# Operand pools moved onto one offset, a fourth pair opened early, 1/rms and the first act moved, own tiles for half-length steps

## The chip, the cores and the metric

The kernel runs on one core of one Trainium2 chip. The metric is the device time of one execution in microseconds. The kernel before takes 2276.01 us (median of 3 runs, 2274.84 to 2279.9). The engines are called as the profile calls them: PE multiplies matrices, PEld loads its weights, DVE, ACT and POOL work on tiles, SP issues the transfers.

## What is computed

One layer of a hybrid network on x of 1024 tokens by 1024 channels, all in float32:

```python
x = x + 0.5 * _swiglu(_rmsnorm(x, ffn1_norm), ffn1_wg, ffn1_wu, ffn1_wd)
h = _rmsnorm(x, mix_norm)
proj = h @ w_in                      # 24 blocks of 128 columns and 32 of gates
# four branches (y_a to y_d), merged with sigmoid gates, then:
x = x + merged @ w_out
x = x + 0.5 * _swiglu(_rmsnorm(x, ffn2_norm), ffn2_wg, ffn2_wu, ffn2_wd)

def _swiglu(x, wg, wu, wd):
    return (silu(x @ wg) * (x @ wu)) @ wd      # 1024 -> 2816 -> 1024
```

## The kernel before

**Numbers in two parts.** Every float32 operand of a large product is split into a rounded part hi and a remainder lo, both in the format float32r: ACT copies hi, DVE (or POOL) subtracts to get lo (`split`, L1010). A product takes three matmuls per block of 128 channels: hi by hi, lo by hi, hi by lo. A matmul has weights of 128x128 (the stationary operand) and 512 columns (the moving operand).

**A feed-forward's first half** (`gate_up`, L1236) runs over 22 pairs f of a gate block and an up block of 128 columns. Each pair's two products (gate and up, two halves of the channels, two halves of the tokens) are computed from seven smaller ones instead of eight, as in Strassen's scheme in Winograd's form: A11, S2, A12, S1, S4, A22, S3 (`NAMES`, L985). Each of the seven is 12 matmuls (`one`, L1154), 84 for a pair. The left operands (the moving ones) come from x, scaled by the norm's gain: A11 and A12 are plain halves of x, S1 to S4 sums and differences of quarters of it. They are made once per feed-forward; A11, A12, S2 and S1 lie in the pools h0 and h1, S3, S4 and A22 in xc (`xc_tiles`, L1015). The right operands (the weights) are made for each pair by `prep_gate` (L1127: g, in pool rg) and `prep_up` (L1136: t in rt, u in ru, v in v), from two loads of 512 KB into the three raw buffers.

`first` (L1166) is A11 and a copy of its result to t by ACT (L1170); `second` (L1173) adds A12 to it and copies it by ACT (L1176); `rest` (L1179) is S2, S1, S4, A22, S3 with DVE's additions. `act` (L1202) multiplies by 1/rms (`scale`), takes silu on ACT and multiplies gate by up on DVE, and every second pair `spill` (L1213) writes seven blocks to memory for the second half.

**The opening.** The norm's 1/rms isn't needed until `act`, so products begin on x itself. `left` (L1426) makes the left operands, and opens pairs 0, 1 and 2, that is, runs their A11 and A12 ahead of S2, since S2 needs sums of x. 1/rms is a background job, `rms` (L1102): 32 matmuls of one column (ms, L1098) give the mean square, `rsqrt` (L148) is a chain of 11 small DVE instructions (L152 to L157) behind one addition (L1108), and 16 matmuls (r, L1116) spread it over the partitions, for two ACT copies to `scale`.

**Background jobs** (`Background`, L65) are generators. Each `one` ticks twice (L1164). A generator yields how many ticks it wants to sleep; `finish` runs it to its end at once. In `rms(2, 7)` the means come at the third tick after it was added, r seven ticks later; `gate_up` calls `finish` after pair 0 (L1250), ahead of its `act`.

**A feed-forward's second half** (`down`, L1257) multiplies the activations with wd, again in seven products. Each runs over six steps of two 128-blocks; the sixth has one block, since 22 pairs make 11 blocks of 256. `factors` (L1291) loads and splits a step's two operands (a from memory, b from wd) into the tiles ahi, alo, dhi, dlo. Steps with an even number in the order of all 42 take the four rg tiles, odd ones two of rt and two of ru, and they are made up to two steps ahead (`get`, L1312).

**The mixers** in between multiply h, in the h0/h1 pools again, with 24 blocks of w_in and 32 of gates (`unit`, L207: 24 matmuls for each half of the tokens), beside background jobs for the branches; `product` (L248) is merged @ w_out, with its moving operands in h0/h1 as well.

**What sets the order.** PE's order is that of the source (L1419 asks for it). The instructions of DVE, ACT, POOL and SP are put in order when the program is built, by a planner with its own estimate of durations, which gives a tile's memory to the next tile of its tag when the last reader is done. Each engine then runs its queue in that order.

**Pools.** SBUF is handed out in the order in which pools are opened (L96 to L100): constants, h0 and h1 (eight tiles of 4096 bytes per partition each), norm, then raw, rg, rt and the rest. The norm pool holds y, t and v of `rsqrt`, two tiles each of 64 bytes per partition. All the large tiles are multiples of 512 bytes.

The functions that the change touches:

Of the kernel before, what the change touches and what calls it, by code (L numbers as in the profile page):

```python
# [11 lines left out]
F32R = mybir.dt.float32r  # L12
# [22 lines left out]
class Weights:  # L35


    def __init__(self, nc, ahead):
        self.nc, self.ahead, self.alloc = nc, ahead, None
        self.src, self.got, self.lo_engine = [], {}, []  # L40
        self.issued = 0
# [51 lines left out]
class Net:  # L93
    def __init__(self, ctx, tc, a, cols):
        self.tc, self.nc, self.a = tc, tc.nc, a
        pool = lambda name, **kw: ctx.enter_context(tc.tile_pool(name=name, **kw))  # L96
        self.cpool = pool("const", bufs=1)
        self.hpools = [pool("h0", bufs=8), pool("h1", bufs=8)]
        self.npool = pool("norm", bufs=1)
        self.wide = {k: pool(k, bufs=b, reuse_waits="tile") for k, b in {"raw": 3, "rg": 4, "rt": 2}.items()}  # L100
        self.w, self.wo = Weights(self.nc, 2), Weights(self.nc, 2)
        self.w.alloc = self.wo.alloc = self.weight
        self.bg = Background()
        nc = self.nc
        self.small = self.const("small")
        self.mean_col = self.column("mean_col")
        nc.gpsimd.memset(self.mean_col, 1.0 / D)
        self.cols = cols
        self.eps = self.column("eps")
        nc.gpsimd.memset(self.eps, EPS)  # L110
# [866 lines left out]
class Ffn:  # L977
# [9 lines left out]
    def __init__(self, net, n, es):  # L987
        self.net, self.nc, self.n = net, net.nc, n
        pool = lambda name, bufs: es.enter_context(
            net.tc.tile_pool(name=f"{name}{n}", bufs=bufs, reuse_waits="tile")  # L990
        )
        sizes = {"xc": 12, "ru": 2, "tt": 1, "a": 3, "u": 1, "scale": 1}
        self.narrow = {k: pool(k, bufs) for k, bufs in {"v": 3, "t": 4, "s": 4}.items()}
        self.wide = net.wide | {k: pool(k, bufs) for k, bufs in sizes.items()}
        self.xc = {}
        self.preps, self.raw_gate = {}, {}
        self.gain = net.col(f"ffn{n}_norm")
        self.ms, self.squares = None, {}
        self.opened = {}
# [51 lines left out]
    def left_cross(self, a11, a21):  # L1051

        for kp in range(2):
            self.nc.vector.tensor_tensor(a11[kp], a11[kp], a21[kp], op=ALU.subtract)
            self.scaled(a11[kp], 2 * kp)
        for kp in range(2):
            self.scaled(a21[kp], 2 * kp)

    def left_s2(self, a11, a22):
        self.s2 = [self.t4("xc", f"S2{kp}") for kp in range(2)]  # L1060
# [1 line left out]
            self.scaled_with(self.s2[kp], a22[kp], 4 + 2 * kp, a11[kp], ALU.subtract)  # L1062
        self.left_split("S2", self.s2)

    def left_rest(self, a11, a12, a21, a22):
        for kp in range(2):
            self.scaled_with(a21[kp], a22[kp], 4 + 2 * kp, a21[kp], ALU.add)
        self.left_split("S1", a21)
        for kp in range(2):
            self.scaled_with(a12[kp], a12[kp], 4 + 2 * kp, self.s2[kp], ALU.subtract)  # L1070
        self.left_split("S4", a12)
        self.left_plain("A22", a22, 4)
        self.left_split("S3", a11)
# [102 lines left out]
        self.nc.scalar.copy(g[:, 0], ps)  # L1176
        return g

    def rest(self, f, t, g, x=None):  # L1179

        nc, net = self.nc, self.net
        V = nc.vector

        def ps_of(name):
            ps = net.ps(f"{name}p{f}")
            self.one(ps, f, name)
            return ps

        V.tensor_tensor(t, ps_of("S2"), t, op=ALU.add)
        if g is None:  # L1190
            g = self.second(f, x)
        w = self.t2("t", f"w{f}")
        V.tensor_tensor(w, ps_of("S1"), t, op=ALU.add)
        u = self.t4("u", f"u{f}")
        V.tensor_tensor(u[:, 0], ps_of("S4"), w, op=ALU.add)
        V.tensor_tensor(g[:, 1], ps_of("A22"), t, op=ALU.add)
        ps = ps_of("S3")
        V.tensor_tensor(g[:, 1], ps, g[:, 1], op=ALU.add)  # L1198
        V.tensor_tensor(u[:, 1], ps, w, op=ALU.add)
        return lambda: self.act(f, g, u)  # L1200

    def act(self, f, g, u):  # L1202
        nc = self.nc
        V = nc.vector
        V.tensor_tensor(g, g, self.scale, op=ALU.mult)  # L1205
        nc.scalar.activation(g, g, AF.Silu)  # L1206
        V.tensor_tensor(u, u, self.scale, op=ALU.mult)
        V.tensor_tensor(g, g, u, op=ALU.mult)
        self.acts[f] = g
        if f % 2:  # L1210
            self.spill(f // 2, self.acts.pop(f - 1), self.acts.pop(f))
# [24 lines left out]
    def gate_up(self, also):  # L1236

        net = self.net
        self.acts = {}
        for f in range(NF):  # L1240
            self.prep_up(f)
            self.prep_gate(f + 1)
            if f in self.opened:
                _, t, g = self.opened.pop(f)
                act = self.rest(f, t, g)
            else:
                x, t = self.first(f)
                act = self.rest(f, t, None, x)
            if f == 0:
                net.bg.finish()  # L1250
            act()
            if f == 2:
                also()

# [2 lines left out]
    def down(self, residual, dst, after):  # L1257
        nc, net = self.nc, self.net
        V, mm = nc.vector, nc.tensor.matmul
        n = NF // 2  # L1260
        steps = (n + 1) // 2
# [5 lines left out]
        def load(kh, nh, s):  # L1267
            w = min(2, n - 2 * s)
            t = self.t4(place[kh, nh][s], f"wd{kh}{nh}{s}")
            src = net.a[f"wd{self.n}"][2 * s : 2 * s + w, kh, nh].rearrange("c p t -> p c t")  # L1270
            nc.sync.dma_start(t[:, :w], src)
            raw[kh, nh, s] = t[:, :w]
# [10 lines left out]
        def right(name, s):  # L1283
            at = {"A11": (0, 0), "S2": (0, 0), "A12": (1, 0), "S4": (1, 1), "S3": (0, 1), "A22": (1, 0)}
            if name != "S1":
                return raw[at[name] + (s,)]
            t = self.t4("tt", f"T1{s}")[:, : raw[0, 0, s].shape[1]]
            V.tensor_tensor(t, raw[1, 1, s], raw[0, 0, s], op=ALU.subtract)
            return t

        def factors(name, s):  # L1291
            w = min(2, n - 2 * s)
            i = order.index((name, s))
            if name == "A11":
                load(0, 0, s)
            a = self.t4("raw", f"in{name}{s}")[:, :w]
            nc.sync.dma_start(a, net.a["acts"][self.NAMES.index(name), 2 * s : 2 * s + w].rearrange("c p t -> p c t"))
            for _ in range(2):
                if i and later:
                    load(*later.pop(0))  # L1300
            b = right(name, s)
            tags = ("rt", "rt", "ru", "ru") if i % 2 else ("rg",) * 4
            hi, lo, bhi, blo = (
                self.t4(tag, f"{what}{name}{s}", F32R)[:, :w] for tag, what in zip(tags, ("ahi", "alo", "dhi", "dlo"))
            )
            bs = self.split(b, bhi, blo)
            return self.split(a, hi, lo), bs

        order = [(name, s) for name in self.NAMES for s in range(steps)]
        ready, summed = {}, set()  # L1310
# [30 lines left out]
        def x_of(q, k):  # L1341
            if (q, k // 2) not in loads:
                x = self.t4(X0[k // 2] if q == 1 else "xc", f"res{q}{k // 2}")
                part = residual[k - k % 2 : k - k % 2 + 2, :, q * TH : (q + 1) * TH].rearrange("k p t -> p k t")
                nc.sync.dma_start(x, part)
                loads[q, k // 2] = x
            return loads[q, k // 2][:, k % 2]
# [21 lines left out]
        for i in range(4):  # L1369
            x = x_of(0, i)  # L1370
# [4 lines left out]
        for i in range(4):  # L1375
            add_half(ws[i], beta[i], ts[i])
            x = x_of(0, 4 + i)
            V.tensor_tensor(x, x, ws[i], op=ALU.add)
        alpha = accumulate("S4", new("D"))
        for i in range(4):  # L1380
            x = x_of(0, 4 + i)
# [4 lines left out]
        for i in range(4):  # L1386
            x = x_of(1, 4 + i)
            V.tensor_tensor(x, x, ws[i], op=ALU.add)
        for i in range(4):
            x = x_of(1, i)  # L1390
            V.tensor_tensor(x, x, ts[i], op=ALU.add)
        beta = accumulate("S3", new("E"))
        for i in range(4):
            x = x_of(1, 4 + i)
            add_half(x, beta[i], x)
            done(1, 4 + i)
            x = x_of(1, i)
# [3 lines left out]
        for i in range(4):  # L1401
            x = x_of(1, i)
# [7 lines left out]
def build(ctx, tc, a, cols):  # L1410
    n = Net(ctx, tc, a, cols)
# [14 lines left out]
    def left(ffn, x0, x1, engine, late):  # L1426

        ffn.open(1)
        for i in range(2):
            ffn.open_second(i)  # L1430
        ffn.left_s2(x0[:2], x1[2:])
        ffn.prep_up(0)
        ffn.open(2)
        ffn.open_second(2)
        ffn.add_squares(engine)
        for q, kp in late:
            ffn.square((x0, x1)[q][kp], q, kp)
            ffn.add_squares(engine)
        ffn.left_rest(x0[:2], x0[2:], x1[:2], x1[2:])
        n.bg.add(ffn.rms(2, 7))  # L1440

    with ExitStack() as es:
        n.psums(es, 8, "f1")
        ffn = Ffn(n, 1, es)
        tags = iter(X0 + ("xc",) * 4)
# [7 lines left out]
        x0 = [load(0, 0)]  # L1453
# [8 lines left out]
        x1 = [load(1, k) for k in range(4)]  # L1462
# [8 lines left out]
    with ExitStack() as es:  # L1471
        n.psums(es, 8, "f2")
        ffn = Ffn(n, 2, es)
        tags = iter(X0 + ("xc",) * 4)
        x = {}
# [109 lines left out]
```

## Time and profile before

| | us |
|---|---|
| median of 3 runs | 2276.01 |
| the profiled execution | 2277.5 |
| its span, first to last instruction | 2275.7 |
| PE busy in the span | 2220.4 |
| DVE busy | 1379.8 |
| ACT busy | 875.5 |
| POOL busy | 327.9 |

The busy time of PE counts a matmul from its start to its modelled end, and neighbours overlap, so that a row's duration (some 390 ns) is longer than the distance between two starts. PEclk is the clock that PE was granted, 1.00 being 2.4 GHz and 0.50 1.2 GHz, as a mean over the stretch. A row of the timeline has start, duration, engine, line, operation, the tile written and the tiles read, their shape and their number, and in brackets how long the engine was idle before and what ended that.

### The profile page before, as it was taken

What the parts mean: (1) busy time and instruction counts of PE and PEld (TensorE: products, weight loads), DVE (VectorE), ACT (ScalarE), POOL (GpSimd) and SP (SyncE); (2) the same over time, 40 slices, a digit from 0 to 9 for tenths busy, and PEclk for the clock granted to TensorE, in tenths of its full rate; (3) what the DMA queues carried; (4) which work ended last, traced back from release to release, by engine and by line L of the source; (5) the groups of instructions that cost most, each with busy time, mean ns of one, the idle gap of its engine ahead of it and who ended that gap; (6) DMA issues with size and microseconds to landing.
All of it is one profiled execution on the core that took longest, in us unless ns stands there. A gap on an engine that the chain in (4) does not pass through costs nothing.

```text
span 2275.7 us, 26198 instructions
## 1 busy us (share of the span) xinstructions
PE 2220.4 (98%) x10144; PEld 1779.5 (78%) x10144; DVE 1379.8 (61%) x1925; ACT 875.5 (38%) x1154; POOL 327.9 (14%) x227
## 2 busy tenths in 40 slices
PE   6899999999999999999999999999999999999999
PEld 5688888887777777787777777888778888888777
DVE  8787777776673436314355233035788787777764
ACT  6232233233443533316477454133433333223332
POOL 0000000000003435223343344321100000000000
PEclk8999999999999999999999999999999999999999
DMA  3233232394333122231111222115223232348432
GB/s 142 93 102 106 86 111 91 124 325 149 106 125 112 53 75 78 77 117 65 58 54 45 74 72 88 47 47 181 79 93 115 93 116 93 116 135 318 139 115 93
DMA packets 115196, 245.10 MB, mean 108 GB/s; under 512 B 11264, under 2 KB 23168, under 8 KB 115072
## 3 DMA queue, kind: packets, MB, share of 16 engines
q1 hardware_dynamic: 115072, 243.44, 32.0%
q8 instruction: 79, 1.29, 0.2%
q14 instruction: 45, 0.37, 0.1%
HBM read 181.00 MB, written 62.39 MB: 107 GB/s over the span
## 4 chain that ended last, share of the span: by engine, by line
PE 91%; DVE 6%; ACT 2%; issue 1%; DMA 0%; POOL 0%; SPq 0%; DVEq 0%; ACTq 0%; POOLq 0%
PE X L1162 3%; PE X L1160 3%; PE X L1161 3%; PE S1p L1160 2%; PE S2p L1162 2%; PE S1p L1162 2%; PE S1p L1161 2%; PE S2p L1161 2%; PE S2p L1160 2%; PE S4p L1161 2%; PE S4p L1160 2%; PE S4p L1162 2%; PE S3p L1162 2%; PE S3p L1161 2%; PE A22p L1161 2%; PE S3p L1160 2%
## 5 line engine op out<-in xcount | busy, mean ns | idle before, releaser
L56 POOL TENSOR_TENSOR wlo<-raw,whi 128x1024 fp32r<-128x1024 f32 x56 | 136.4, 2438 | 258.3 <-ACT whi L55 246.7
L1011 ACT ACTIVATE uhi<-gu 128x1024 fp32r<-128x1024 f32 x44 | 46.7, 1062 | 276.4 <-PE S3p L1161 134.4
L55 ACT ACTIVATE whi<-raw 128x1024 fp32r<-128x1024 f32 x72 | 76.0, 1057 | 186.4 <-PE o L261 23.5
L964 DVE TENSOR_TENSOR gt<-gt,wb 128x512 f32<-128x512 f32 x48 | 32.9, 686 | 139.8 <-PE wb L956 80.0
L1011 ACT ACTIVATE ghi<-gu 128x1024 fp32r<-128x1024 f32 x44 | 46.7, 1060 | 164.4 <-DMA gu<-wgu 129.8
L191 POOL TENSOR_TENSOR nm0lo<-res,nm0hi 128x1024 fp32r<-128x1024 f32 x2 | 4.9, 2444 | 648.9 <-ACT nm0hi L190 648.9
L1160 PE MATMUL X<-A11hi,ghi 128*128 128x512 f32 x176 | 71.1, 404 | 9.3 <-ACT ghi L1011 9.3
L965 POOL TENSOR_TENSOR m<-m,gt 128x512 f32<-128x512 f32 x48 | 62.3, 1299 | 122.6 <-DVE gt L964 121.7
L1012 DVE TENSOR_TENSOR dloS<-wd,dhiS 128x1024 fp32r<-128x1024 f32 (+1 forms) x36 | 43.1, 1196 | 59.6 <-ACT dhiS L1011 59.6
L1160 PE MATMUL X<-A12hi,ghi 128*128 128x512 f32 x176 | 70.8, 402 | 7.7 <-ACT t L1170 7.7
L1162 PE MATMUL X<-A11hi,glo 128*128 128x512 f32 x176 | 71.5, 406 | 6.6 <-DVE glo L1012 6.6
L1011 ACT ACTIVATE dhiA<-wd 128x1024 fp32r<-128x1024 f32 (+1 forms) x36 | 35.6, 990 | 107.3 <-PE Ad L1332 53.4
L1011 ACT ACTIVATE dhiS<-wd 128x1024 fp32r<-128x1024 f32 (+1 forms) x36 | 35.6, 989 | 106.9 <-PE Dd L1332 39.1
L1162 PE MATMUL S2p<-S2hi,tlo 128*128 128x512 f32 x176 | 70.2, 399 | 4.2 <-DVE tlo L1012 4.2
L1206 ACT ACTIVATE a<-a 128x1024 f32<-128x1024 f32 x44 | 46.7, 1062 | 65.3 <-DVE a L1205 65.3
L1160 PE MATMUL S1p<-S1hi,thi 128*128 128x512 f32 x176 | 70.7, 402 | 0.0
L1161 PE MATMUL X<-A11lo,ghi 128*128 128x512 f32 x176 | 70.5, 401 | 0.0
L1162 PE MATMUL S1p<-S1hi,tlo 128*128 128x512 f32 x176 | 70.5, 400 | 0.0
L1161 PE MATMUL S1p<-S1lo,thi 128*128 128x512 f32 x176 | 70.4, 400 | 0.0
L1161 PE MATMUL X<-A12lo,ghi 128*128 128x512 f32 x176 | 70.4, 400 | 0.0
L1198 DVE TENSOR_TENSOR a<-S3p,a 128x512 f32<-128x512 f32 x44 | 30.4, 691 | 66.0 <-PE S3p L1162 66.0
L1332 PE MATMUL Ad<-aloA,dhiA 128*128 128x512 f32 x176 | 68.7, 390 | 1.6 <-DVE aloA L1012 1.6
(1209 smaller groups left out, 6895.1 us busy)
## 6 DMA issues: line engine op xcount, KB each, us to landing
gu<-wgu SPq DMA_DIRECT2D x92, 512.0 KB, 3.6
raw<-w_in SPq DMA_DIRECT2D x56, 512.0 KB, 3.5
acts<-s SPq DMA_DIRECT2D x88, 256.0 KB, 2.8
wd<-wd SPq DMA_DIRECT2D x40, 512.0 KB, 6.5
inS<-acts SPq DMA_DIRECT2D x40, 512.0 KB, 3.7
acts<-a SPq DMA_DIRECT2D x66, 256.0 KB, 3.3
inA<-acts SPq DMA_DIRECT2D x30, 512.0 KB, 3.7
res<-x SPq DMA_DIRECT2D x16, 512.0 KB, 7.1
```

What stands on the lines that cost most here:

```text
L55: nc.scalar.activation(hi, raw, AF.Copy)
L56: getattr(nc, self.lo_engine[i]).tensor_tensor(lo, raw, hi.bitcast(F32), op=ALU.subtract)
L964: nc.vector.tensor_tensor(g, g, ps, op=ALU.mult)
L965: nc.gpsimd.tensor_tensor(m, m, g, op=ALU.add)
L1011: self.nc.scalar.activation(hi, src, AF.Copy)
L1012: self.nc.vector.tensor_tensor(lo, src, hi.bitcast(F32), op=ALU.subtract)
L1160: mm(ps, whi[:, s], hi, start=start and k == 0, stop=False, skip_group_check=True)
L1161: mm(ps, whi[:, s], lo, start=False, stop=False, skip_group_check=True)
L1162: mm(ps, wlo[:, s], hi, start=False, stop=k == 3, skip_group_check=True)
L1198: V.tensor_tensor(g[:, 1], ps, g[:, 1], op=ALU.add)
L1206: nc.scalar.activation(g, g, AF.Silu)
L1332: mm(outs[t], whi[:, j, m], alo[:, j], start=False, stop=False, skip_group_check=True)
```

## The change

1. The norm pool is opened ahead of h0 and h1 instead of behind them.
2. Four pairs are opened instead of three; the t pool has five tiles instead of four. The first half of S1's making (a21 times the gain) moves from `left_cross` to a new `left_s1`, called ahead of the sums of squares.
3. `rms(2, 7)` becomes `rms(4, 7)`. `rest` calls `mid` behind S1 for the opened pairs, and `mid` is `acts`: it finishes the background and runs the acts that wait. Pair 0's act is not run behind pair 0 any more.
4. In `down`, a step of one block takes three tiles of v and one of t; the steps of two blocks alternate between rg and rt/ru by their own count. a is split ahead of b.

```diff
         self.cpool = pool("const", bufs=1)
+        self.npool = pool("norm", bufs=1)
         self.hpools = [pool("h0", bufs=8), pool("h1", bufs=8)]
-        self.npool = pool("norm", bufs=1)
...
-        self.narrow = {k: pool(k, bufs) for k, bufs in {"v": 3, "t": 4, "s": 4}.items()}
+        self.narrow = {k: pool(k, bufs) for k, bufs in {"v": 3, "t": 5, "s": 4}.items()}
...
             self.scaled(a11[kp], 2 * kp)
-        for kp in range(2):
-            self.scaled(a21[kp], 2 * kp)
...
-    def left_rest(self, a11, a12, a21, a22):
+    def left_s1(self, a21, a22):
         for kp in range(2):
+            self.scaled(a21[kp], 2 * kp)
             self.scaled_with(a21[kp], a22[kp], 4 + 2 * kp, a21[kp], ALU.add)
         self.left_split("S1", a21)
+
+    def left_rest(self, a11, a12, a22):
...
-    def rest(self, f, t, g, x=None):
+    def rest(self, f, t, g, x=None, mid=lambda: None):
...
         V.tensor_tensor(w, ps_of("S1"), t, op=ALU.add)
+        mid()
...
         self.acts = {}
+        waiting = []
+
+        def acts():
+            net.bg.finish()
+            while waiting:
+                waiting.pop(0)()
+
         for f in range(NF):
             self.prep_up(f)
             self.prep_gate(f + 1)
             if f in self.opened:
                 _, t, g = self.opened.pop(f)
-                act = self.rest(f, t, g)
+                waiting.append(self.rest(f, t, g, mid=acts))
             else:
                 x, t = self.first(f)
-                act = self.rest(f, t, None, x)
-            if f == 0:
-                net.bg.finish()
-            act()
+                waiting.append(self.rest(f, t, None, x))
+            if f:
+                acts()
...
-            tags = ("rt", "rt", "ru", "ru") if i % 2 else ("rg",) * 4
-            hi, lo, bhi, blo = (
-                self.t4(tag, f"{what}{name}{s}", F32R)[:, :w] for tag, what in zip(tags, ("ahi", "alo", "dhi", "dlo"))
-            )
-            bs = self.split(b, bhi, blo)
-            return self.split(a, hi, lo), bs
+            what = [f"{x}{name}{s}" for x in ("ahi", "dhi", "alo", "dlo")]
+            if w == 1:
+                hi, bhi, lo, blo = (
+                    self.t2(tag, x, F32R).rearrange("p (a b) -> p a b", a=1) for tag, x in zip(("v", "v", "v", "t"), what)
+                )
+            else:
+                full = i - i // steps
+                tags = ("rt", "rt", "ru", "ru") if full % 2 else ("rg",) * 4
+                hi, bhi, lo, blo = (self.t4(tag, x, F32R) for tag, x in zip(tags, what))
+            return self.split(a, hi, lo), self.split(b, bhi, blo)
...
         for i in range(2):
             ffn.open_second(i)
+        ffn.open(2)
         ffn.left_s2(x0[:2], x1[2:])
         ffn.prep_up(0)
-        ffn.open(2)
-        ffn.open_second(2)
+        ffn.open(3)
+        for i in (2, 3):
+            ffn.open_second(i)
+        ffn.left_s1(x1[:2], x1[2:])
         ffn.add_squares(engine)
...
-        ffn.left_rest(x0[:2], x0[2:], x1[:2], x1[2:])
-        n.bg.add(ffn.rms(2, 7))
+        ffn.left_rest(x0[:2], x0[2:], x1[2:])
+        n.bg.add(ffn.rms(4, 7))
```

## Rows read from the trace of the kernel before

**Rows 1.** The page's first part: busy us, share of the span and instructions of each engine.
```profile
PE 2220.4 (98%) x10144; PEld 1779.5 (78%) x10144; DVE 1379.8 (61%) x1925; ACT 875.5 (38%) x1154; POOL 327.9 (14%) x227
```

**Rows 2.** Stretches: length; busy PE, PEld, DVE, ACT, POOL; PEclk, DMA share, GB/s.
```profile
0.00:50.00 50.00, 31.07 (x117) 23.38 (x117) 44.89 (x85) 36.09 (x48) 0.34 (x6) 0.89 0.44 161
50.00:100.00 50.00, 43.23 (x182) 35.81 (x182) 37.40 (x59) 15.28 (x17) 0.00 (x0) 0.87 0.22 79
...
200.00:250.00 50.00, 50.00 (x218) 40.61 (x217) 41.55 (x54) 15.65 (x20) 0.00 (x0) 1.00 0.36 123
...
1600.00:1650.00 50.00, 45.35 (x203) 36.36 (x202) 41.12 (x51) 22.59 (x27) 5.13 (x2) 0.97 0.24 74
1650.00:1700.00 50.00, 47.36 (x207) 38.51 (x206) 42.26 (x60) 17.76 (x20) 0.00 (x0) 0.97 0.33 105
```

**Rows 3.** PE's groups by form, 120 to 460 us: count | busy us, mean ns | idle.
```profile
L1160 PE MATMUL S2p<-S2hi,thi 128*128 128x512 f32 x72 | 28.4, 395 | 0.0
...
L1160 PE MATMUL S3p<-S3hi,uhi 128*128 128x512 f32 x71 | 27.6, 389 | 0.0
```

**Rows 4.** Timeline of PE, 200 to 222 us, one steady pair.
```profile
202.24 0.40 PE L1160 MATMUL S2p<-S2hi,thi 128*128 128x512 f32 x1
...
210.63 0.39 PE L1160 MATMUL S4p<-S4hi,uhi 128*128 128x512 f32 x1
...
213.37 0.39 PE L1160 MATMUL A22p<-A22hi,vhi 128*128 128x512 f32 x1
...
218.81 0.40 PE L1160 MATMUL X<-A11hi,ghi 128*128 128x512 f32 x1
```

**Rows 5.** Timeline of PE, 1450 to 1458 us: twelve of a unit, then the next.
```profile
1449.78 0.40 PE L215 MATMUL gb2q<-nm1hi,whi 128*128 128x512 f32 x1
...
1452.58 0.39 PE L954 MATMUL wb<-ybhi,wbhi 128*128 128x512 f32 x1
```

**Rows 6.** PE's groups by form over the whole span: the output product.
```profile
L260 PE MATMUL o<-mhi,whi 128*128 128x512 f32 x128 | 50.6, 395 | 0.0
```

**Rows 7.** Timeline, 555 to 566 us: a joint between two products of down.
```profile
562.28 1.22 DVE L1012 TENSOR_TENSOR aloS<-inS,ahiS 128x1024 fp32r<-128x1024 f32 x1
...
562.38 0.39 PE L1331 MATMUL Cd<-ahiS,dhiS 128*128 128x512 f32 x1
...
563.56 0.50 PE L1332 MATMUL Cd<-aloS,dhiS 128*128 128x512 f32 x1 [0.79 <-DVE aloS L1012]
563.90 0.40 PE L1333 MATMUL Cd<-ahiS,dloS 128*128 128x512 f32 x1
```

**Rows 8.** Waits of PE, 0 to 130 us: us in total, times, longest.
```profile
PE r L1116 <- DVE f1rs_y L157: 6.8, 1, 6.8
PE X L1162 <- DVE glo L1012: 5.9, 3, 4.9
...
PE S2p L1162 <- DVE tlo L1012: 1.5, 1, 1.5
```

**Rows 9.** Waits of PE, 1600 to 1710 us.
```profile
PE X L1160 <- ACT t L1170: 3.9, 2, 2.4
PE S2p L1162 <- DVE tlo L1012: 2.6, 1, 2.6
```

**Rows 10.** Timeline of DVE, first opening: the chain's first and last instruction.
```profile
54.70 0.16 DVE L1108 TENSOR_SCALAR v<-ms 128x8 f32<-128x8 f32 x1
...
69.74 0.16 DVE L157 SCALAR_TENSOR_TENSOR f1rs_y<-f1rs_t,f1rs_y 128x8 f32<-128x8 f32 x1
```

**Rows 11.** Timeline of DVE, second opening: first, two in the middle, last.
```profile
1643.30 0.17 DVE L1108 TENSOR_SCALAR v<-ms 128x8 f32<-128x8 f32 x1 [3.21 <-PE ms L1098]
...
1650.57 0.17 DVE L155 TENSOR_TENSOR f2rs_t<-f2rs_y 128x8 f32<-128x8 f32 x1
1650.77 0.17 DVE L156 SCALAR_TENSOR_TENSOR f2rs_t<-f2rs_t,v 128x8 f32<-128x8 f32 x1
...
1652.26 0.16 DVE L157 SCALAR_TENSOR_TENSOR f2rs_y<-f2rs_t,f2rs_y 128x8 f32<-128x8 f32 x1
```

## The prediction

> **What bounds the kernel now.** The page comes first: PE is busy for 2220.4 us of 2275.7 [rows 1], so the time is what the matmuls take plus some 55 us in which PE stands. The table by stage says where it stands [rows 2]: in the first 100 us (18.9 and 6.8 us) and again where the second feed-forward opens (4.6 and 2.6 us), there also at a lower granted clock (0.89 and 0.87, then 0.97), while 200 to 250 us shows 50.00 of 50.00 at 1.00, with DVE at 41.6. So a change gains either where PE stands or in what one matmul takes, and I asked for both.
>
> A matmul's duration overlaps its neighbour's, so the cost of one is the distance between starts. In a steady pair, the 36 matmuls from 202.24 to 210.63 (S2, A12, S1) are 233.1 ns apart, and the 24 of A22 and S3, from 213.37 to 218.81, 226.7 ns [rows 4]. The groups by form say the same as 395 and 389 ns [rows 3]. All have 128x128 weights, 512 columns and the full clock. What sets the 395 ns group apart is the pool of the moving operand: A11, A12, S2, S1 lie in h0/h1, those of 389 ns in xc. The mixers' units, whose moving operand lies in h0/h1 too, show 2.80 us for 12, that is 233.3 ns [rows 5], and the output product 395 ns [rows 6].
>
> **The change, part by part.** The sum is made against the profiled execution (2277.5 us, span 2275.7). It stands 1.5 us above the median of 2276.0, and I give the result against the median.
>
> *1. The norm pool ahead of h0/h1.* It holds six tiles of 16 floats, 384 bytes. Before, h0/h1 lie ahead of it and every other operand pool behind it, so the two operands of the 395 ns group differ by 384 bytes (less whole multiples of 512), and those of the other by none. Afterwards none differ. The group counts: 2 feed-forwards x 22 pairs x 4 products x 12 = 2112; 56 units x 2 halves x 24 = 2688; the product 2x2x4x24 = 384; together 5184. At 233.1 - 226.7 = 6.4 ns that is 33.2 us. In the two openings (4 pairs each, 384 matmuls) other engines set the pace, so I count 4800: **-30.7 us**. The units of [rows 5] follow each other without a gap, so I let their 2688 count in full. Bounds: 0 (the cause is something else about these pools) and -33.2. I take the upper part, because down draws both operands from several pools and its first row in [rows 7] is 0.39 us long as well, so the weights' pool isn't the cause. What remains open is whether it's the offset or the place of h0/h1 itself.
> The trace has two speeds for one shape [rows 4]. The Trainium skill, "TensorE: Matmul & The Clock Gate", section "Step-by-step: what each phase is for", says that PE reads SBUF through two independent ports, one for the moving operand and one for the weights. By that, where the two lie should not matter, and this term would be 0.
>
> *2. Own tiles for down's half-length steps.* Each product of down ends in a step of one block (12 matmuls, 2.7 us instead of 5.4), and the next product's first step needs the tiles of the step before that. Its alo is written last: DVE starts it at 562.28, PE has begun at 562.38, and the second matmul comes at 563.56, 1.18 us after the first, with 0.34 more behind it, instead of 2 x 0.227 [rows 7]. That is 1.06 us. The same stands at each of the six joints of either feed-forward, 12 in all: 12.7 us. With v, v, v, t for the half step and the parity counted over full steps, the next full step takes tiles that came free one step earlier, 5.4 us. Then DVE's two splits (1.22 us each [rows 7]) fit, and ACT's two, which run beside them. The order a before b makes alo earlier by one more. One of the 12 joints lies beside the first feed-forward's norm, where DVE and POOL are taken by it, and may stay: **-12 us** (-8 to -13). What hides the added tile: t has five, four hold dt, and v is free in down.
>
> *3. The openings.* (a) A fourth pair's A11 and A12, 24 matmuls or 5.6 us, come ahead of the first S2. They don't go away: they are taken from pair 3. They are worth what they cover, at most the waits in the X matmuls: 5.9 us on glo in the first opening [rows 8], 3.9 us on ACT's copy of t in the second [rows 9]. But A11 of pair 3 needs its own glo, behind pair 0's up part on DVE, where pair 2's stood before: I take half, -5 us in all. Its cost on the queues: one more 512 KB load per feed-forward on SP's queue (the opened gate is read again) and one more split at prep time that was done later before. A fourth gate result finds no free tile of a (three) until pair 0's spill is out, so one of eight PSUM banks stays taken till then; a pair needs five: 0. (b) The four scalings of a21 no longer stand ahead of the t copies on ACT's queue: -2, of the 4.8 us that (a) leaves of these waits. On POOL, which adds the squares in the second opening, nothing is added: 0. (c) tlo is late at the first unopened pair: PE waits 1.5 us and 2.6 us at S2 [rows 8, 9]. DVE and the three raw buffers then run behind, since an opened pair has only 60 matmuls, 13.8 us. That wait moves one pair on: 0.
> (d) *1/rms.* By its name it comes later. I read the code otherwise. rms(4, 7) gets its first four ticks from S2 and S1 of pair 0, which leave its counter at 1. Then pair 0's own mid() drains the background, with nothing waiting yet. So the 32 small ms matmuls and r stand on PE together, between S1 and S4 of pair 0, and PE waits for the whole chain on DVE. Behind r stand S4, A22, S3 of pair 0 and all that DVE and ACT make of them. Price: the chain's first instruction to its last took 15.0 us in the first opening, with other work of DVE between its steps, and 9.0 in the second [rows 10, 11]; where nothing came between, a step took 0.20 us [rows 11], and 11 steps 2.2. Before, 42 matmuls (9.8 us) lay between, and r waited 6.8 us and none. In its place now stand between 2 and 15 us in each. I take 6 and 5, since DVE has less left to do then and the splits of S1 come earlier. What it gives back: the 6.8 us. A standing PE also pays with its clock: 0.87 over 50 us means 13 us at 1.2 instead of 2.4 GHz, 6.5 us lost [rows 2]. The first opening has such stretches already, the second gets one more like its present one (0.97 over 50 us: 3 us at the lower level, 1.5 lost), about 2 us. (e) The first act, three DVE instructions of 1.22 us, goes behind S1 of pair 1; its transfers leave with pair 1's as before. PE's 13.8 us per pair cover it: 0.
> Sum of 3: -5 + (6 - 6.8) + 5 + 2, about +1; with (b) **-1 us**, from -21 (every wait of rows 8 and 9 gone, no new one) to +21 (15.0 + 9.0 - 6.8 + 4 for the clock, and nothing gained).
>
> Sum: -30.7 - 12 - 1 = -44, so 2276 - 44 = **2232 us**.
>
> **Rivals.** *A. The offset is not the cause* (h0/h1's own region is, or what reads them): part 1 gives 0, 2276 - 13 = 2263 us. For it: no row shows h0/h1 at the other offset. Against: two speeds that follow the pool in three stages [rows 3 to 6]. 0.12. (The Trainium skill's two ports, cited above, would make it this one.) *B. The drained chain costs its whole length*: 15 and 9 us and 4 for the clock, while (a) and (b) still give 7: part 3 comes to +14, and the time to 2248 us. For it: before, DVE put other work between the steps. Against: with PE standing, DVE runs out of such work. 0.14. *C. The openings go as they are meant to*: glo, t, r and tlo waits all vanish, 5.9 + 6.8 + 1.5 + 3.9 + 2.6 = 20.7: 2276 - 30.7 - 12 - 20.7 = 2213 us. That needs the chain to be short, 0.11. *D. Slower: DVE's new order.* The order of DVE's queue is planned anew. If in the steady pairs an act's 3.7 us stood ahead of tlo, as at pair 3 now, each of the 36 unopened pairs would lose 1.5 to 2.6 us [rows 8, 9], 54 to 94 us: 2286 to 2326 us. It decides from 44/36 = 1.2 us per pair. Against: DVE is busy for 41.6 of 50 us with PE never waiting [rows 2], and a pair takes 19.0 us afterwards, against 16.1 of DVE. 0.05.
>
> **How the numbers follow.** The forecast has 0.58, with a range of its own of 2221 to 2243. A and D lie outside of 2212 to 2254, the rest within. About 0.2% (4.6 us) is what a measurement of this kernel can tell from no change. A, B, C and the forecast are all faster by more; D is slower. A and B together would come to 2276 - 12 + 14 = 2278, about 0.12 x 0.14 = 0.02 for the same: faster 0.93, same 0.02, slower 0.05.
>
> **What would show it.** Part 1: X, S1, S2 at 389 ns and starts 226.7 ns apart, units and o alike; 395 would be A. Part 2: no wait on alo at the first step of a product. Part 3: ms and r next to each other between S1 and S4 of pair 0, a PE wait on f1rs_y of 2 to 15 us in both openings, and the wait on tlo at S2 of pair 4. The prediction is wrong if r stands behind pair 0, if the h0/h1 matmuls keep their distance, or if steady pairs show waits of PE.

## The result, and the profile after

The changed kernel takes 2249.47 us (median of 4 runs, 2247.78 to 2251.35) against 2276.67 us (2274.84 to 2279.9) of the kernel before in the same series: a ratio of 0.9879, 95% interval 0.9862 to 0.9896, or 27.2 us less. The forecast was 44 us less. The profiled execution took 2247.78 us with a span of 2246.0, 29.7 less than before. Where they lie, by the starts of the same PE instructions in both traces:

| stretch of PE | before, us | after, us | change |
|---|---|---|---|
| first X to the last matmul of pair 3 | 7.62 to 121.75 | 7.60 to 122.32 | +0.6 |
| to the first matmul of down (18 pairs) | to 470.58 | to 465.27 | -5.9 |
| first down, to the first unit | to 693.99 | to 677.29 | -11.4 |
| mixers, to the output product | to 1523.62 | to 1496.17 | -10.8 |
| output product | to 1613.21 | to 1583.21 | -2.6 |
| second opening, to the last matmul of pair 3 | to 1707.28 | to 1689.41 | +12.1 |
| to the first matmul of down (18 pairs) | to 2056.10 | to 2032.35 | -5.9 |
| second down, to the end | to 2275.70 | to 2245.97 | -6.0 |

The page's first part answers to [rows 1]: PE is busy for 28.7 us less; the others differ by under 3 us.

```profile
PE 2191.7 (98%) x10144; PEld 1782.3 (79%) x10144; DVE 1377.5 (61%) x1925; ACT 873.0 (39%) x1154; POOL 327.3 (15%) x227
```

The table by stage answers to [rows 2], with the same columns.

```profile
0.00:50.00 50.00, 36.04 (x136) 27.54 (x136) 43.27 (x82) 34.63 (x46) 0.34 (x6) 0.93 0.49 172
50.00:100.00 50.00, 39.59 (x181) 33.60 (x181) 37.90 (x60) 17.36 (x22) 0.00 (x0) 0.86 0.23 76
200.00:250.00 50.00, 50.00 (x223) 41.39 (x222) 42.15 (x55) 16.09 (x20) 0.00 (x0) 1.00 0.34 121
1600.00:1650.00 50.00, 41.39 (x184) 34.48 (x183) 31.62 (x50) 17.15 (x22) 0.00 (x0) 0.83 0.19 62
1650.00:1700.00 50.00, 46.20 (x193) 37.22 (x192) 44.81 (x60) 15.71 (x18) 0.00 (x0) 0.93 0.38 126
```

In 200 to 250 us PE fits 223 matmuls in where it had 218. In 1600 to 1650, in the second opening, which begins 30 us earlier than before, it stands for 8.6 us, and its clock is 0.83.

PE's groups by form, 120 to 460 us, answer to [rows 3]; the timeline rows under them to [rows 4]; then the output product over the whole span, to [rows 6].

```profile
L1161 PE MATMUL S3p<-S3hi,uhi 128*128 128x512 f32 x72 | 28.0, 389 | 0.0
...
L1163 PE MATMUL X<-A11hi,glo 128*128 128x512 f32 x72 | 28.0, 389 | 0.0
L1161 PE MATMUL S2p<-S2hi,thi 128*128 128x512 f32 x72 | 28.0, 389 | 0.0
```
```profile
201.43 0.39 PE L1161 MATMUL S2p<-S2hi,thi 128*128 128x512 f32 x1
...
202.11 0.39 PE L1161 MATMUL S2p<-S2hi,thi 128*128 128x512 f32 x1
```
```profile
L260 PE MATMUL o<-mhi,whi 128*128 128x512 f32 x128 | 49.8, 389 | 0.0
```

The two speeds are gone: all groups show 389 ns, and three S2 matmuls take 0.68 us, 227 ns each. The joint between two products of down [rows 7] has no wait left:

```profile
555.19 0.39 PE L1343 MATMUL Cd<-ahiS,dhiS 128*128 128x512 f32 x1
555.41 0.39 PE L1344 MATMUL Cd<-aloS,dhiS 128*128 128x512 f32 x1
```

The waits of PE in the openings, first 0 to 130 us [rows 8], then 1575 to 1700 us [rows 9]:

```profile
PE X L1161 <- ACT ghi L1011: 11.1, 3, 7.6
PE r L1117 <- DVE f1rs_y L157: 10.4, 1, 10.4
PE X L1163 <- DVE glo L1012: 2.9, 4, 1.8
PE S2p L1163 <- DVE tlo L1012: 2.2, 1, 2.2
PE S2p L1161 <- ACT thi L1011: 1.9, 1, 1.9
```
```profile
PE r L1117 <- DVE f2rs_y L157: 4.6, 1, 4.6
PE X L1161 <- ACT t L1171: 2.6, 1, 2.6
PE X L1163 <- DVE glo L1012: 2.6, 2, 1.8
PE X L1161 <- ACT ghi L1011: 2.1, 1, 2.1
PE S2p L1161 <- ACT thi L1011: 1.9, 1, 1.9
PE S2p L1163 <- DVE tlo L1012: 1.9, 1, 1.9
```

In the first opening glo went from 5.9 to 2.9 us and ACT's t from 3.8 to nothing, while ghi went from 9.3 to 11.1: X waits 14.0 us in all instead of 19.0. In the second, X waits 7.3 us instead of 4.7 (0.8 of that for glo), and ghi is new there. These are the two rows of before, 0 to 130 us, that [rows 8] leaves out:

```profile
PE X L1160 <- ACT ghi L1011: 9.3, 2, 7.6
PE X L1160 <- ACT t L1170: 3.8, 2, 3.1
```

The wait for r grew in the first opening, from 6.8 to 10.4, and is new in the second; the wait for thi in S2 is new in both. PE's timeline shows where r stands, and DVE's the chain (answering to [rows 10]):

```profile
48.33 3.63 PE L1099 MATMUL ms<-mean_col,sq 128*128 128x1 f32 x32
62.37 3.78 PE L1117 MATMUL r<-c_ident,f1rs_y 128*128 128x128 f32 x16 [10.41 <-DVE f1rs_y L157]
65.80 0.77 PE L1161 MATMUL S4p<-S4hi,uhi 128*128 128x512 f32 x1
```
```profile
51.36 2.73 DVE L1030 SCALAR_TENSOR_TENSOR A22lo<-n1x,c_small,A22hi 128x512 fp32r<-128x512 f32 x4
54.01 2.35 DVE L1012 TENSOR_TENSOR S3lo<-n0x,S3hi 128x1024 fp32r<-128x1024 f32 x2
...
56.88 0.15 DVE L1109 TENSOR_SCALAR v<-ms 128x8 f32<-128x8 f32 x1
...
62.14 0.17 DVE L157 SCALAR_TENSOR_TENSOR f1rs_y<-f1rs_t,f1rs_y 128x8 f32<-128x8 f32 x1
```

1/rms doesn't come later. ms and r stand on PE between S1 and S4 of pair 0, as the code was read, and the means, done at 51.96, wait for DVE's splits of A22 and S3 before the chain begins.

### The profile page after: what moved, and what is told of

It reads as the page before. It is cut to its first block, busy times and chain, and to the rows that moved or that the text cites. A ratio compares the mean times of both kernels' runs of the same rounds, so it can differ in the third digit from the quotient of the medians.

```text
span 2246.0 us, 26117 instructions
## 1 busy us (share of the span) xinstructions
PE 2191.7 (98%) x10144; PEld 1782.3 (79%) x10144; DVE 1377.5 (61%) x1925; ACT 873.0 (39%) x1154; POOL 327.3 (15%) x227
## 4 chain that ended last, share of the span: by engine, by line
PE 89%; DVE 6%; ACT 2%; issue 2%; POOL 1%; DMA 0%; SPq 0%; POOLq 0%; ACTq 0%; DVEq 0%
PE X L1163 3%; PE X L1161 3%; PE X L1162 3%; PE S2p L1163 2%; PE S2p L1161 2%; PE S2p L1162 2%; PE S4p L1161 2%; PE Ad L1345 2%; PE S4p L1163 2%; PE S1p L1161 2%; PE S4p L1162 2%; PE Ad L1344 2%; PE S1p L1162 2%; PE S1p L1163 2%; PE Ad L1343 2%; PE S3p L1161 2%
## 5 line engine op out<-in xcount | busy, mean ns | idle before, releaser
L1011 ACT ACTIVATE ahiS<-inS 128x1024 fp32r<-128x1024 f32 (+1 forms) x48 | 46.9, 989 | 131.3 <-PE Dd L1344 31.7
L1012 DVE TENSOR_TENSOR aloS<-inS,ahiS 128x1024 fp32r<-128x1024 f32 (+1 forms) x48 | 54.5, 1135 | 60.9 <-ACT ahiS L1011 60.9
L1161 PE MATMUL X<-A11hi,ghi 128*128 128x512 f32 x176 | 71.9, 409 | 13.2 <-ACT ghi L1011 13.2
L1161 PE MATMUL S2p<-S2hi,thi 128*128 128x512 f32 x176 | 70.2, 399 | 3.8 <-ACT thi L1011 3.8
L1162 PE MATMUL S2p<-S2lo,thi 128*128 128x512 f32 x176 | 70.1, 399 | 0.0
L1161 PE MATMUL S4p<-S4hi,uhi 128*128 128x512 f32 x176 | 69.4, 394 | 0.0
L1162 PE MATMUL S4p<-S4lo,uhi 128*128 128x512 f32 x176 | 68.7, 391 | 0.0
L1163 PE MATMUL S4p<-S4hi,ulo 128*128 128x512 f32 x176 | 68.7, 390 | 0.0
L1345 PE MATMUL Ad<-ahiA,dloA 128*128 128x512 f32 x176 | 68.7, 390 | 0.0
```

What stands on the lines that cost most here:

```text
L1011: self.nc.scalar.activation(hi, src, AF.Copy)
L1012: self.nc.vector.tensor_tensor(lo, src, hi.bitcast(F32), op=ALU.subtract)
L1161: mm(ps, whi[:, s], hi, start=start and k == 0, stop=False, skip_group_check=True)
L1162: mm(ps, whi[:, s], lo, start=False, stop=False, skip_group_check=True)
L1163: mm(ps, wlo[:, s], hi, start=False, stop=k == 3, skip_group_check=True)
L1345: mm(outs[t], wlo[:, j, m], ahi[:, j], start=False, stop=last, skip_group_check=True)
```

## The experiments

Each is compared with the kernel before on its own chip; a gain is the difference of those two medians.

**Each part alone, and the change without its openings.** e1 swaps the two lines of the pools and no more:

```diff
+        self.npool = pool("norm", bufs=1)
         self.hpools = [pool("h0", bufs=8), pool("h1", bufs=8)]
-        self.npool = pool("norm", bufs=1)
```

> The kernel before with the norm pool ahead of h0 and h1 and nothing else. My theory: the offset between the two operands sets 226.7 or 233.1 ns between starts, so this edit alone gives what the comparison of the two traces shows in the steady pairs (36 x 0.33 = 12 us), the mixers (11 us) and the output product (2.6 us), about -25 us, and the S2 and X matmuls show 389 ns. Rival: the shorter matmuls came with another part of the change (other orders, other tiles), and this edit alone gives within 3 us of nothing, with 395 ns as before.

2252.74 us, ratio 0.9895 (0.9878 to 0.9912): 23.2 us less. S2, X and o show 389 ns. By the same starts as in the table, the two times 18 pairs give 5.9 us each, the output product 2.6, the mixers 8.4 and the two openings 2.3 and 0.7; the first down is 2.8 us longer, at a mean clock of 0.98 where before had 1.00. This edit alone does it; the rival falls.

e2 takes only the last hunk of the change, `factors`, and `"t": 5`.

> The kernel before with down's own tiles for the steps of one block (and a split ahead of b, five t tiles) and nothing else. My theory: the wait for alo goes at all joints, and the stretches of down become as short as the two traces show, 11.4 and 6.2 us: -17 us. Rival: only the waits that the prediction counted go, 12 x 1.06 = -12 us, and the rest of what down gained came from other parts of the change.

2258.77 us, 0.992 (0.9905 to 0.9934): 17.2 us less. In its trace the second down is 6.2 us shorter, that is 1.03 us for each of six joints, nearly the 1.06 that the prediction gave one. The first is 9.3 us shorter: from E's first matmul to F's first, beside the norm, it is 3.7 us less, where another product gives some 1.1. Its second opening is 3.7 us shorter as well, with a clock of 0.98 against 0.96 there; no part of the prediction has that.

e3 is the kernel before with parts 2 and 3 of the change's list (openings, 1/rms, act, `"t": 5`).

> The kernel before with the new openings alone: four pairs opened, S1's first half later, 1/rms and the first act moved, five t tiles. My theory: PE stands behind S1 of pair 0 for the whole chain of 1/rms in both openings, and this part costs what the two traces show, 0.6 + 12.1 = +13 us. Rival, the prediction's own term: -1 us, and the loss in the openings comes from how the new orders meet the other two parts.

2293.75 us, 1.0074 (1.0058 to 1.0091): 17.8 us more. By itself this part makes the kernel slower, and its waits are those of the changed kernel (r 10.1 and 4.6 us). By starts its two openings cost 0.3 and 12.6 us, near what my theory said; 5.0 more are lost in the mixers.

e4 is the other half, e1 and e2 together, with the openings of before.

> The changed kernel with the openings of before: norm pool first and own tiles, three pairs opened, 1/rms as before. My theory: the two parts add up and nothing is given back, -25 - 17 = -42 us against before, about 2234 us, some 15 us faster than the changed kernel. Rival: the openings' loss stays although their edit is gone, because the orders of DVE and ACT are planned anew, and it comes out within 5 us of the changed kernel's 2249 us.

2235.59 us (2230.97 to 2238.41), 0.9816 (0.9799 to 0.9833): 40.3 us less, where e1 and e2 sum to 23.2 + 17.2 = 40.4. The two parts add up, and the openings cost the changed kernel 40.3 - 27.2 = 13 us; by starts e4's second opening is 1.7 us shorter than before's, where the changed kernel's is 12.1 longer. The interval lies wholly below the changed kernel's.

**Which part of the openings costs it.** All of these have e1's and e2's edits. In e5 the call behind S1 of pair 0 leaves the background alone:

```diff
         def acts():
-            net.bg.finish()
+            if waiting:
+                net.bg.finish()
```

> The changed kernel, but the call behind S1 of pair 0 finishes the background only when an act waits for it, so that 1/rms runs at its ticks: means in S4 of pair 0, r at the end of S2 of pair 1. My theory: the early draining is what makes PE stand (r waits 10.4 and 4.6 us); 42 matmuls then lie between means and r as before, both waits go almost, and it gains 10 to 14 us on the changed kernel, to about 2237 us. Rival: the chain comes late on DVE wherever r stands, the wait only moves to r at its new place, and it gains at most 3 us.

2241.83 us, 0.9848 (0.9832 to 0.9864): 34.2 us less, 7 better than the changed kernel. No wait for r is left, but a new one, PE on ACT's thi, 5.1 us at S2 of pair 1 in the first opening. The gain lies between the two theories: r's waits went, as mine had it, and the new one took 5.1 of their 15.0 us back.

e6 has the four pairs and S1's later half, but `rms(2, 7)`, and finishes and acts behind pair 0 as before.

> Norm pool, own tiles, four pairs opened and S1's first half later, but 1/rms and the first act as before. My theory: four pairs alone cost about 6 us, nearly all in the second opening, where gate splits stand on ACT's queue behind S1, u and t (X phase 10.4 us longer for 5.5 us of work), so about 2242 us, 6 above the kernel without the new openings (2235.6). Rival: all of the openings' loss is the drained chain, and this comes out at 2231 to 2236 us, as the prediction's -5 and -2 for these edits would have it.

2240.4 us, 0.9842 (0.9827 to 0.9857): 35.6 us less, 4.7 worse than e4.

e7 is the converse, three pairs with the drained 1/rms (the edit against e4):

```diff
         V.tensor_tensor(w, ps_of("S1"), t, op=ALU.add)
+        mid()
...
+                waiting.append(self.rest(f, t, g, mid=acts))
...
-        n.bg.add(ffn.rms(2, 7))
+        n.bg.add(ffn.rms(4, 7))
```

> Norm pool, own tiles, three pairs opened as before, but 1/rms and the first act as in the changed kernel, drained behind S1 of pair 0. My theory: the drained chain costs 1 us net in the first opening and 6 in the second, so about 2243 us, 7 above the kernel without the new openings. Rival: with three pairs opened DVE has more left to do when the chain is asked for, and it costs the 14 us of the whole difference, 2249 us.

2242.56 us, 0.9851 (0.9837 to 0.9866): 33.5 us less, 6.9 worse than e4. With 4.7 from e6 that is 11.6 of the 13. The interval of e7 lies above e4's; that of e6 overlaps it a little.

e11 is e6 with S1's first half where it was before, so that the fourth pair is alone:

> Norm pool, own tiles and four pairs opened, but S1's first half, 1/rms and the first act as before. My theory: the fourth pair alone costs the 5 us, since its split of g stands on ACT's queue ahead of what S2 needs or behind it, so about 2240 us as with S1 moved. Rival: the move of S1's first half costs them (S1's splits come ahead of g's on ACT), and without it this is 2231 to 2235 us, the -5 that the prediction gave the fourth pair.

2242.0 us, 0.9848 (0.9832 to 0.9864): 33.7 us less, 6.6 worse than e4, with an interval that just touches e4's. The traces say where: by starts e11 is 1.0 us shorter than e4 in the first opening and 8.7 longer in the second. So it is the fourth pair by itself that costs time there; S1's move gives back 1.9, which these intervals (some 3.7 us to either side) can't tell from nothing.

Why a fourth pair costs time shows in the changed kernel's second opening. Rows of PE's timeline in 1580 to 1640 us, then DVE's and ACT's beside them:

```profile
1603.17 0.53 PE L1161 MATMUL X<-A11hi,ghi 128*128 128x512 f32 x1 [2.15 <-ACT ghi L1011]
1605.97 0.80 PE L1163 MATMUL X<-A11hi,glo 128*128 128x512 f32 x1 [1.84 <-DVE glo L1012]
1630.22 3.78 PE L1117 MATMUL r<-c_ident,f2rs_y 128*128 128x128 f32 x16 [4.61 <-DVE f2rs_y L157]
```
```profile
1594.17 1.21 DVE L1012 TENSOR_TENSOR S2lo<-S,S2hi 128x1024 fp32r<-128x1024 f32 x1
...
1599.44 1.21 DVE L1012 TENSOR_TENSOR tlo<-tt,thi 128x1024 fp32r<-128x1024 f32 x1
...
1601.18 2.34 DVE L1012 TENSOR_TENSOR S1lo<-o1x,S1hi 128x1024 fp32r<-128x1024 f32 x2
...
1604.71 1.21 DVE L1012 TENSOR_TENSOR glo<-gu,ghi 128x1024 fp32r<-128x1024 f32 x1
```
```profile
1601.06 0.59 ACT L1171 COPY t<-X 128x512 f32<-128x512 f32 x1 [1.77 <-PE X L1163]
...
1602.07 1.05 ACT L1011 ACTIVATE ghi<-gu 128x1024 fp32r<-128x1024 f32 x1
```

S2 of pair 0 needs S2lo and tlo: both are done by 1600.65. But on PE A11 of pair 3 stands ahead of it, and that waits until 1603.17 for ghi, whose split stands on ACT behind the copy of pair 2's t, and until 1605.97 for glo, behind S1lo on DVE. The early pair doesn't fill PE's wait; it puts work that isn't ready ahead of work that is. In e4 PE waits only for t there, 2.58 and 1.02 us. e11 has the same two new waits, 2.1 us for ghi and 1.6 for glo.

**1/rms at its ticks, with three pairs.** e8 is e7 with e5's edit.

> Norm pool, own tiles, three pairs opened as before, 1/rms four ticks in and finished only when an act waits, the first act behind S1 of pair 1. My theory: this is what the move of 1/rms can give by itself, the 6.8 us wait on f1rs_y of the first opening, so about 2229 us, faster than both kernels. Rival: the later act pushes DVE's tlo of pair 3, PE waits there instead, and it stays at 2234 to 2238 us.

2237.25 us (2226.69 to 2240.4), 0.9833 (0.9817 to 0.985): 38.8 us less, not better than e4. Its trace has no wait for r, but this one (waits of PE, 0 to 130 us; then DVE's timeline):

```profile
PE S2p L1160 <- ACT thi L1011: 5.1, 1, 5.1
```
```profile
56.38 0.16 DVE L1108 TENSOR_SCALAR v<-ms 128x8 f32<-128x8 f32 x1
56.57 0.69 DVE L1196 TENSOR_TENSOR u<-S4p,w 128x512 f32<-128x512 f32 x1
...
65.23 0.68 DVE L1146 TENSOR_TENSOR tt<-gu,tt 128x512 f32<-128x512 f32 x1
```

The additions of pair 0 and the chain now lie ahead of pair 1's tt on DVE, and thi needs tt. The rival's number came, by a wait that neither theory had named: thi of pair 1, not tlo of pair 3.

e12 is e8 with `left_s1` as in the change.

> Norm pool, own tiles, three pairs opened, 1/rms at its ticks, the first act behind S1 of pair 1, and S1's first half later as in the changed kernel. My theory: S1's move takes four scalings off ACT's queue ahead of the copies of t and gives the 2 us that the prediction gave it, about 2235 us against 2237 without it, faster than both kernels. Rival: it puts S1's splits where gate splits are waited for and costs 2 us or more, 2239 us and up.

2236.2 us, 0.9824 (0.9809 to 0.9838): 39.5 us less, 0.7 better than e8, which is within the spread. e4, e8 and e12 (2235.6 to 2237.3) all beat both kernels and can't be told apart; e4 is the simplest.

**What about the offset makes the two speeds.** e9 shifts every pool behind norm by two tiles of 64 bytes:

```diff
         self.npool = pool("norm", bufs=1)
+        self.ppool = pool("pad", bufs=1)
         self.hpools = [pool("h0", bufs=8), pool("h1", bufs=8)]
...
+        for i in range(2):
+            nc.gpsimd.memset(self.ppool.tile([P, LINE], F32, tag=f"pad{i}", name=f"pad{i}")[:, :1], 0.0)
```

> The changed kernel with 128 bytes of padding behind the norm pool: h0/h1 lie at 256 modulo 512, where they lay before, and all other operand pools are shifted by as much, so the two operands of a product still differ by nothing modulo 512. My theory: only the difference between the two operands counts; X, S2, S1 and the units stay at 389 ns, and the time is the changed kernel's, 2249 us. Rival: the place of h0/h1 itself sets the speed, and they show 395 ns again, some 25 us more.

One run, 2251.98 us. PE's groups by form, 120 to 460 us:

```profile
L1166 PE MATMUL X<-A11hi,glo 128*128 128x512 f32 x72 | 28.0, 389 | 0.0
L1166 PE MATMUL S2p<-S2hi,tlo 128*128 128x512 f32 x72 | 28.0, 389 | 0.0
```

The h0/h1 pools lie where they lay before, and their matmuls are short all the same: the place itself doesn't matter. e10 puts y and t of the norm, 256 bytes, behind h0/h1 and leaves v ahead:

```diff
         self.hpools = [pool("h0", bufs=8), pool("h1", bufs=8)]
+        self.npool2 = pool("norm2", bufs=1)
...
-        return self.npool.tile([P, LINE], F32, tag=tag, name=name, bufs=bufs)[:, :w]
+        at = self.npool2 if tag[-1] in "yt" else self.npool
+        return at.tile([P, LINE], F32, tag=tag, name=name, bufs=bufs)[:, :w]
```

> The changed kernel with two of the norm pool's three pairs of tiles behind h0/h1 and one ahead, so that the operands differ by 256 bytes modulo 512 instead of by nothing (the kernel before: by 128). My theory: any difference makes them slow, X, S2, S1 and the units show 395 ns, and it takes about 25 us more than the changed kernel, 2274 us. Rival: only the distance of before is slow, and they stay at 389 ns.

One run, 2249.49 us, and the same view shows

```profile
L1163 PE MATMUL X<-A11hi,ghi 128*128 128x512 f32 x72 | 28.0, 389 | 0.0
...
L1163 PE MATMUL S2p<-S2hi,thi 128*128 128x512 f32 x72 | 28.0, 389 | 0.0
```

My theory falls in this form: operands 256 bytes apart are as fast as operands that are alike. What is shown is that 384 bytes between the pools (counted the other way round, 128 modulo 512) are slow and that 0 and 256 are fast. Other distances weren't tried, so the rule behind it stays open.

## Why the prediction was right, and where it was wrong

The sign held, and 2249 lies between the 2212 and 2254 that hold the forecast with B and C. It lies outside of the forecast's own 2221 to 2243: that missed by 17 us. Term by term:

| term | predicted | measured | from |
|---|---|---|---|
| 1, norm pool | -30.7 | -23.2 | e1 |
| 2, own tiles | -12 | -17.2 | e2 |
| 3, openings | -1 | +13.1 | e4 against the changed kernel |
| 3a, fourth pair | -5 | +6.6 | e11 against e4 |
| 3b, S1's half later | -2 | -1.9, -0.7 (not resolved) | e6 against e11, e12 against e8 |
| 3d, 1/rms | +6 - 6.8 + 5 + 2 = +6.2 | +6.9 | e7 against e4 |

**Term 1** was right in its cause and in the size of one matmul. Where PE is fed without a gap the gain came whole: 18 pairs gave 5.9 us, the output product 2.6 (384 x 6.4 ns = 2.5). The step that failed is "I let their 2688 count in full". Of those 17.2 us the mixers gave 8.4 in e1 and 10.8 in the changed kernel. PE's order there is the same in all three traces, so that each distance between two starts can be compared. Of the units' matmuls, 2585 have less than 260 ns to the next start both before and after the change; they came 5.1 ns closer, not 6.4, 13.2 us in all. Of these, 2.4 are lost again: PE stands for 5.9 us instead of 3.3, and these two waits for DVE are new in the changed kernel (waits of PE, 677 to 1496 us).

```profile
PE nm1ms L167 <- DVE work L205: 0.9, 1, 0.9
PE p0q L216 <- DVE nm1lo L191: 0.6, 1, 0.6
```

In e1 the clock takes a share as well: three units come 1.5, 1.9 and 1.7 us later behind the unit ahead of them than they did before, and what comes ahead of two of them lies in these windows, in which before had a clock of 1.00:

```profile
850.00:860.00 10.00, 9.92 (x66) 7.52 (x65) 9.32 (x24) 3.67 (x7) 6.44 (x5) 0.87 0.17 66
...
890.00:910.00 20.00, 19.83 (x105) 14.70 (x103) 13.21 (x38) 3.88 (x6) 9.65 (x7) 0.91 0.19 66
```

The Trainium skill, "TensorE: Matmul & The Clock Gate", section "Step-by-step: what each phase is for", lets PE read both operands through independent ports, from which the prediction drew that this term would be 0. e1 doesn't agree with that: 23.2 us came from moving 384 bytes.

**Term 2** was right in mechanism, to 1.03 against 1.06 us per joint in the second down. The joint that "may stay" didn't: beside the norm PE had more to lose than at the others, and the first down gave 3.1 us more than the second. Some of e2's 17.2 us isn't the joints: the two downs gave 15.5, and the shorter second opening has a part in it.

**Term 3a is the step that failed**, "I take half, -5 us in all". In the first opening it held as far as it went: X waited 5.0 us less, 24 more X matmuls fit ahead of S2, and S2 of pair 0 began at 42.89 us instead of 42.51. But what pair 3 no longer had to do was lost again at its own S2. In the second opening X didn't fill waits but made them, as the rows above show. Of the 8.7 us that e11 loses there against e4, 3.7 are the waits for ghi and glo and 2.5 more waiting at pair 3's S2, with 1.0 less for t; the other 3.5 fit the clock, 0.92 in the mean of that stretch against 0.94. I had priced the waits that a fourth pair could cover, and not that its own splits come last on two queues. One gain I didn't see either: the first down takes 212.0 us with four pairs opened and 214.1 with three (the changed kernel and e4), because PE no longer waits 1.9 us for ACT at the first unit; why ACT is ready sooner is open.

**Term 3c**, "that wait moves one pair on: 0", was wrong in place and size. It stayed at pair 3, although that pair was opened, with thi added to tlo: 1.9 + 2.2 us and 1.9 + 1.9, against 1.5 and 2.6, and a slow stretch behind it. A likely reason, not tested: its A11, 12 matmuls or 2.7 us, no longer stands between pair 2 and its S2.

**Term 3d** was right in place and sign; that its sum fits is partly luck. In the first opening r waited 10.4 us in the changed kernel and 8.6 in e7, where I took 6; in the second 4.6 in both, where I took 5. The 2 us for the clock don't show: by starts e7's openings are 0.9 and 4.9 us longer than e4's, 5.8 in all, where r's waits alone come to 8.6 - 6.8 + 4.6 = 6.4.

**The rivals.** A fell with e1, and h0/h1's own place as the cause with e9; D didn't come: no steady pair waits. B gave 2248 us, and 2249 was measured, but not for B's reason: the drained chain costs 6.9 us and not the +21 that B's +14 was made of; the fourth pair made up the rest, and terms 1 and 2 missed in opposite directions. A total that fits can hide two errors, and only e6, e7 and e11 told them apart. C would have needed a chain without a wait; e5 and e8 have that, and the wait came up elsewhere.

**The clock** is what 2 us in the sum stood for. One stall and what follows it, pair 3 in the first opening (windows with the columns of [rows 2]; then PE's timeline):

```profile
100.00:105.00 5.00, 2.97 (x12) 1.80 (x10) 4.97 (x8) 2.25 (x3) 0.00 (x0) 1.00 0.08 32
105.00:112.00 7.00, 4.95 (x12) 3.91 (x13) 5.15 (x6) 1.44 (x2) 0.00 (x0) 0.51 0.21 78
```
```profile
107.05 0.80 PE L1163 MATMUL S2p<-S2hi,tlo 128*128 128x512 f32 x1 [2.16 <-DVE tlo L1012]
...
108.07 0.63 PE L1162 MATMUL S2p<-S2lo,thi 128*128 128x512 f32 x1
...
111.06 0.63 PE L1163 MATMUL S2p<-S2hi,tlo 128*128 128x512 f32 x1
```

PE waits twice, 1.9 us for thi and 2.2 for tlo; behind that the clock is at its lower level, 1.2 GHz, and from 108.07 to 111.06 lie seven distances of 427 ns instead of 227, 1.4 us more in these alone. The Trainium skill, "TensorE: Matmul & The Clock Gate", section "Wait — 56ns, not 53.3ns?", gives 426.7 ns at this level, which these rows bear out, and about 215.7 at the full one, where the steady rows here have 227. Over the span, one minus the mean clock times the length is 2275.7 x 0.008 = 18 us before and 2246.0 x 0.012 = 27 us after: by this estimate up to 9 of the missing 17 us went with the lower clock. It is an upper bound, since time in which PE stands is counted in it as well, and it is a part of the terms above, not one beside them.

## What to carry to other kernels

When two speeds show for one shape of matmul, look at which pool each operand lies in and at the bytes of small pools between them. Work opened early helps only if its own operands are ready before the work it is put ahead of; look at where its splits stand on the queues of DVE and ACT, not only at the wait it is meant to fill. A call that finishes background work at once must ask whether anyone waits, and a wait taken out of a full queue should be expected one instruction further on.

## What was not expected of the hardware

- Products with the two operands 128 bytes apart modulo 512 started 233.1 ns apart, with 0 or 256 bytes 226.7 ns.
- The executions of e8 differ mainly in their clock. Five had spans of 2224.9, 2235.1, 2238.6, 2235.5 and 2235.5 us at mean clocks of 0.995, 0.990, 0.989, 0.989 and 0.989: span times clock is 2211 to 2214 us in all of them, where the last digit of the clock is worth 2 us. So a gain of a few us at a stall can be drowned by whether the clock fell behind it. By the same product the profiled executions have 2257 (before, 2275.7 x 0.992), 2219 (changed) and 2212 (e4).
